# Squaring the second block's token rows two feature tiles after their load, at a fixed place in ScalarE's order

## The chip, the cores and the metric

The kernel runs on one core of a Trainium2 chip. The metric is the device time of one execution in microseconds (us); of several runs of a kernel the median counts. The engines are named as the profile names them: PE is TensorE (matrix products), PEld its weight loads, DVE is VectorE, ACT is ScalarE, POOL is GpSimd, SP is SyncE, which here issues all transfers (its rows read SPq). Each engine works through its own list of instructions in order and waits on semaphores for the others.

## The reference

One layer of a diffusion backbone is computed for 128 context tokens and 2048 latent tokens, of 1024 features each, in float32. Cut to what matters here:

```python
h = rmsnorm(x, norm_mix) * (1.0 + sc1) + sh1          # adaLN-modulated norm of each token row
proj = h @ w_in                                       # q, k, v (512 each), gate, betas and decays, gMLP parts
qkv = silu(centred_conv(proj[..., :1536], conv))      # 3-tap convolution along the tokens
q, k = l2norm(q per head), l2norm(k per head)         # 4 heads of 128
o_a  = gated delta rule over chunks of 64, both directions
o_b  = gelu(u) * (spatial mixing of layernorm(gelu(vg)))
x = x + ga1 * (concat(o_a, o_b) @ w_out)
x = x + ga2 * (relu(rmsnorm(x) * (1 + sc2) + sh2 @ w_ff1) ** 2 @ w_ff2)
y = rmsnorm(x, norm_final)
```

The norm needs, for each token row, the sum of the squares of its 1024 features. That sum is what the change moves.

## The kernel before

The 17 tiles of 128 tokens are worked off in phases. The **first phase** (to about 430 us) makes q, k and v of all tokens, their convolution and the products k k^T and q k^T; then follow the scans of the delta rule with the gMLP part and the output projection, and from about 1200 us the feed-forward part. Products that must be exact are made three times: an operand is split into a rounded part (names in H) and a rest (names in L), and `mm3` issues H*H, L*H and H*L (lines 241 to 243).

The first phase goes through six **blocks** of three tiles (the last has two): `BLOCKS`. Within a block there are twelve **feature tiles**, each 128 of the 1536 q, k and v features for all 384 tokens of the block: 24 matmuls into one PSUM bank (`pj`, three banks), then the convolution (`convolve`: a scaled copy on ACT at L568 and two multiply-adds on DVE at L571 read the bank, then a tanh on ACT at L574 and a product on DVE at L575 into a tile x2), one step later a transposition on PE (L584, into one of three banks `pt`) and its evacuation on ACT (squares at L595 and L601, a copy at L588), and later further transposes and products (L614, L625, L628).

Beside the matmuls of feature tile n of a block, side steps for the **next block** are issued. They are listed by `prep_block`, one entry of its list `first` per feature tile:

- entries 0 to 2, `load_x`: allocate one of three buffers with the tag x, load one tile of token rows (512 KB, L462) and at once issue the square with its row sum on ACT (L467, `junk<-x`);
- entries 3 to 5: `columns_r` (the inverse root of the sums and a diagonal matrix of it), `rows_r` (a product with ones that spreads it over the partitions, L481, copied at L484), and the loads of three pairs of transposed feature rows (`load_pair`, L491, 384 KB each, into the same three buffers with the tag x, so each waits until the square has read its buffer);
- entries 7 to 11 of the feature tiles: `column(k)` for the eight k. Each scales a feature row (DVE, L526), rounds it (ACT, L528, kH) and takes the rest (DVE, L529, kL). A fourth pair is loaded with column 2. Feature tiles of the next block multiply exactly these kH and kL.

So the first block's feature tiles stand beside the preparation of the **second block** (bi == 1 in `prep_block`), the second block's beside the third's, and so on. Beside all this run the casts and differences of the weights (`split_w`, L201 and L202; the v weights are loaded through a ring of four buffers) and the multiply-adds for the modulation vectors (L271, `acc`).

The code gives the steps in program order (`interleave` spreads the side steps evenly between the matmuls). The order of each engine's list is then made by the tile framework's scheduler, which estimates when each instruction could start and puts the lists in that order; it also deals out the rotating buffers. So a step that is written elsewhere can move rows on every engine for some distance behind it. `tc.add_manual_dep` with `NoSync` is a constraint on that scheduler only: one instruction has to stand behind another of the same engine.

## Time and profile before

| what | value |
|---|---|
| runs | 2576.61 us median of 3 (2570.27 to 2578.84) |
| the profiled execution | 2574.76 us, of which the span of its instructions is 2573.0 us |
| PE busy | 2536.3 us of 2573.0 (99%), 15268 matmuls |
| DVE, ACT, POOL busy | 1830.8, 1260.1 and 229.3 us |
| granted TensorE clock, mean | 0.998 |
| transfers | 588.66 MB, 229 GB/s on average |

A row of the timeline gives the start in us from the span's beginning, the duration, the engine, the line, the operation, output<-input without buffer numbers, sizes, and in brackets how long the engine had been idle before and who ended that idle time. Consecutive rows of one kind are merged (x3), and the start of the next row of an engine tells when it took up new work; the durations overlap a little, since an engine overlaps the end of one instruction with the start of the next. A row of windows gives for one stretch its length and then the busy time of PE, PEld, DVE, ACT and POOL with instruction counts, the granted clock, the busy share of the transfer engines and the rate. A row of waits gives the engine and what it waited to do, who released it, the total, the number of times and the longest.

### The profile page before, as it was taken

To read this page: it belongs to the slowest core of one execution; us is meant where nothing else is said; L and a number is where in the kernel's file an instruction comes from. 1 tells how busy PE (TensorE), PEld (TensorE's weight loads), DVE (VectorE), ACT (ScalarE), POOL (GpSimd) and SP (SyncE) were. 2 spreads that over 40 slices of the span, in tenths; PEclk is the share of its full clock that TensorE was granted. 3 is DMA by queue.
4 is the path that set the end of the run, shared out by engine and by line. 5 is a ranking of instruction groups with operands and counts; after the bars stand their busy time and mean duration, and the time that the engine had idled before them with its cause. 6 is when DMAs were issued, how large, how long until landed. Compare 5 with 4: busy or idle time off the path is not lost.

```text
span 2573.0 us, 44472 instructions
## 1 busy us (share of the span) xinstructions
PE 2536.3 (99%) x15268; PEld 2136.7 (83%) x15268; DVE 1830.8 (71%) x3790; ACT 1260.1 (49%) x3119; POOL 229.3 (9%) x448
## 2 busy tenths in 40 slices
PE   9999999999999999999999999999999999999998
PEld 5999999788888788778888888888888887888887
DVE  5867756776676878885678877777675556785875
ACT  4755556555555767763355544444342433243442
POOL 3112212211110111110000000000000000000000
PEclk9999999999999999999999999999999999999999
DMA  8977737744445657785867789665589979776673
GB/s 286 310 215 212 212 114 245 248 160 148 145 155 166 213 190 247 253 280 183 292 199 245 238 281 348 195 180 172 146 272 374 334 263 314 256 258 205 221 264 112
DMA packets 503912, 588.66 MB, mean 229 GB/s; under 512 B 36148, under 2 KB 298588, under 8 KB 500102
## 3 DMA queue, kind: packets, MB, share of 16 engines
q1 hardware_dynamic: 503686, 585.82, 69.7%
q8 instruction: 120, 1.97, 0.3%
q14 instruction: 106, 0.87, 0.1%
HBM read 406.01 MB, written 179.67 MB: 228 GB/s over the span
## 4 chain that ended last, share of the span: by engine, by line
PE 56%; DVE 3%; DMA 3%; ACT 1%; issue 1%; SPq 0%; POOL 0%; POOLq 0%; DVEq 0%; ACTq 0%
PE f L243 16%; PE f L241 16%; PE f L242 16%; PE pd L1026 2%; PE pj L241 1%; PE pj L242 1%; PE pj L243 1%; DMA QK<-qk_d 1%; DMA raw<-in_w_ff_dram 1%; DVE opL L904 0%; DMA kT<-kT_d 0%; DMA h_d<-ev 0%; DVE o L1358 0%; DVE KK L1067 0%; DMA zraw<-z_d 0%
## 5 line engine op out<-in xcount | busy, mean ns | idle before, releaser
L243 PE MATMUL f<-hop,zL 128*128 128x512 f32 (+1 forms) x976 | 377.0, 387 | 1.8 <-DVE zL L1551 1.8
L241 PE MATMUL f<-hop,zH 128*128 128x512 f32 (+1 forms) x976 | 376.9, 387 | 1.2 <-ACT zH L1557 1.2
L242 PE MATMUL f<-hop,zH 128*128 128x512 f32 (+1 forms) x976 | 376.7, 386 | 0.0
L241 PE MATMUL f<-hop,wH 128*128 128x512 f32 x896 | 349.7, 391 | 1.6 <-ACT p L1630 1.6
L242 PE MATMUL f<-hop,wH 128*128 128x512 f32 x896 | 348.7, 389 | 0.0
L243 PE MATMUL f<-hop,wL 128*128 128x512 f32 x896 | 347.3, 389 | 0.0
L1557 ACT CAST zH<-zraw 128x512 fp32r<-128x512 f32 x240 | 146.8, 620 | 295.6 <-DVE zraw L1551 84.2
L243 PEld LDWEIGHTS f<-hop,zL 128*128 128x128 f32 x976 | 183.6, 188 | 39.5 <-DVE zL L1551 3.0
L241 PEld LDWEIGHTS f<-hop,zH 128*128 128x128 f32 x976 | 183.7, 188 | 38.7 <-ACT zH L1557 1.6
L242 PEld LDWEIGHTS f<-hop,zH 128*128 128x128 f32 x976 | 183.7, 188 | 37.7 <-DVE hop L1551 0.3
L1551 DVE TENSOR_TENSOR zL<-zraw,zH 128x512 fp32r<-128x512 f32 x240 | 163.3, 689 | 68.8 <-ACT zH L1557 55.7
L241 PEld LDWEIGHTS f<-hop,wH 128*128 128x128 f32 x896 | 168.2, 188 | 37.3 <-ACT p L1630 3.1
L243 PEld LDWEIGHTS f<-hop,wL 128*128 128x128 f32 x896 | 168.2, 188 | 35.5
L242 PEld LDWEIGHTS f<-hop,wH 128*128 128x128 f32 x896 | 168.3, 188 | 34.6
L241 PE MATMUL pj<-kH,wH 128*128 128x386 f32 (+2 forms) x568 | 190.5, 338 | 1.8 <-ACT junk L601 1.1
L243 PE MATMUL pj<-kH,wL 128*128 128x386 f32 (+2 forms) x568 | 189.7, 335 | 0.0
L242 PE MATMUL pj<-kL,wH 128*128 128x386 f32 (+2 forms) x568 | 189.4, 335 | 0.0
L184 POOL TENSOR_TENSOR r<-rsq,nhalf 128x1 f32<-128x1 f32 (+1 forms) x37 | 23.0, 622 | 1398.1 <-DVE rsq L183 1398.1
L571 DVE SCALAR_TENSOR_TENSOR cv<-pj,vec,cv 128x384 f32<-128x384 f32 (+2 forms) x164 | 87.1, 540 | 53.3 <-ACT cv L568 52.0
L1557 ACT CAST wH<-s 128x512 fp32r<-128x512 f32 x96 | 59.4, 621 | 124.7 <-DVE s L1551 118.2
L241 PEld LDWEIGHTS pj<-kH,wH 128*128 128x128 f32 x568 | 107.1, 189 | 5.3 <-issue 2.1
L202 DVE TENSOR_TENSOR wL<-raw,wH 128x512 fp32r<-128x512 f32 x120 | 81.1, 685 | 38.8 <-ACT wH L201 38.6
(423 smaller groups left out, 5793.6 us busy)
## 6 DMA issues: line engine op xcount, KB each, us to landing
zraw<-z_d SPq DMA_DIRECT2D x212, 256.0 KB
raw<-in_w_ff_dram SPq DMA_DIRECT2D x192, 256.0 KB
hop<-hop_d SPq DMA_DIRECT2D x28, 1024.0 KB
z_d<-c SPq DMA_DIRECT2D x96, 256.0 KB
zraw<-s_d SPq DMA_DIRECT2D x96, 256.0 KB
raw<-in_w_mod_dram SPq DMA_DIRECT2D x80, 256.0 KB
r<-in_w_ff_dram SPq DMA_DIRECT2D x80, 256.0 KB
s_d<-s SPq DMA_DIRECT2D x64, 256.0 KB
```

The source lines that it names most:

```text
L184: G.tensor_tensor(out=out, in0=t[:np_, :n], in1=nhalf[:np_, :n], op=ALU.pow)
L202: V.tensor_tensor(out=lo, in0=raw, in1=f32(h), op=ALU.subtract)
L241: T.matmul(ps, lh, rh, start=first and i == 0, stop=False, skip_group_check=more)
L242: T.matmul(ps, lh, rl, start=False, stop=False, skip_group_check=more)
L243: T.matmul(ps, ll, rh, start=False, stop=last and i == n - 1, skip_group_check=more)
L571: V.scalar_tensor_tensor(out=cv[:, o : o + m], in0=ps[:, s + sh : s + sh + m], scalar=convw[:, w, j : j + 1], in1=cv[:, o : o + m], op0=AL ...
L1026: T.matmul(p[:, h, :], lhs[:, h, :], rhs[:, h, :], start=True, stop=True)
L1551: V.tensor_tensor(out=out, in0=a, in1=b, op=op)
L1557: A.copy(h, src)
```

## The change

For the second block alone (bi == 1) the square is taken out of `load_x`. Its three squares become steps of their own: the first stands at the third feature tile of the first block, in the same step as the third load; the second and third stand at the fourth and fifth. `columns_r`, `rows_r` and the pair loads, which come behind them in the list, thereby move two feature tiles on. In addition each of the three squares is bound to stand behind the ACT instruction that was emitted last before it in the program. For all other blocks the square follows its load as it did.

```diff
@@ load_x, in prep_block
                 load(out=x, in_=xrow(t))
-                if t == tiles[0]:
+                rows.append(x)
+                if bi > 1:
+                    square(t - tiles[0])
+
+            rows = []
+
+            def square(i):
+                if i == 0:
                     xs.append(smp.tile([P, 3], F32, tag="ss3", name="xss"))
-                i = t - tiles[0]
+                last = [x for x in tc.nc.cur_bb.bb.instructions if x.engine == mybir.EngineType.Activation][-1]
                 junk = p1.tile([P, D], BF16, tag="junk", name="junk", bufs=1)
-                A.activation(junk, x, AF.Square, accum_out=xs[0][:, i : i + 1])
+                A.activation(junk, rows[i], AF.Square, accum_out=xs[0][:, i : i + 1])
+                if bi == 1:
+                    tc.add_manual_dep(tc.nc.cur_bb.bb.instructions[-1], last.name, mybir.DependencyInfo(
+                        mybir.DependencyClass.NoSync, mybir.DependencyReason.DATA), reason="order")
...
             first = [lambda t=t: load_x(t) for t in tiles]
+            if bi == 1:
+                last_x = first[2]
+                first = first[:2] + [lambda: (last_x(), square(0)), lambda: square(1), lambda: square(2)]
             if bi:
                 first += [lambda: (columns_r(), load_pair(0)), lambda: (rows_r(), load_pair(1)), lambda: load_pair(2)]
```

No instruction is added or removed. What moves is shown at three places, by each engine's list. The line numbers of the changed kernel are 10 to 13 higher behind the edit (the square is its L474); the numbers behind the names count the buffers.

**ACT, beside the first block's fourth to sixth feature tiles.** cv is the convolution's input, copied out of its bank; x2 the tanh; wH the cast of a v weight that was loaded into raw; junk_... xss the square of token rows; junk2 the square of transposed features. Before:

```order
L574 ACTIVATE x2_845<-cv_844 128x384
L467 ACTIVATE junk_857,xss_856<-x_854 128x1024
L568 ACTIVATE cv_981<-pt_567,vec_195 128x128
L568 ACTIVATE cv_981<-pt_567,vec_195 128x256
L574 ACTIVATE x2_920<-cv_919 128x384
L467 ACTIVATE junk_914,xss_856<-x_912 128x1024
L568 ACTIVATE cv_1079<-pj_1009,vec_195 128x128
L201 CAST wH_949<-raw_947 128x512
L568 ACTIVATE cv_1079<-pj_1009,vec_195 128x256
```

Changed:

```order
L587 ACTIVATE x2_845<-cv_844 128x384
L581 ACTIVATE cv_977<-pt_567,vec_195 128x128
L581 ACTIVATE cv_977<-pt_567,vec_195 128x256
L587 ACTIVATE x2_915<-cv_914 128x384
L581 ACTIVATE cv_1069<-pj_1005,vec_195 128x128
L581 ACTIVATE cv_1069<-pj_1005,vec_195 128x256
L201 CAST wH_944<-raw_942 128x512
L587 ACTIVATE x2_978<-cv_977 128x384
L201 CAST wH_953<-raw_951 128x512
L614 ACTIVATE junk2_928,ss3_929<-pt_924 128x128
L474 ACTIVATE junk_972,xss_971<-x_854 128x1024
```

The first square has moved nine rows down, behind the casts of two v weights; the copies of the third and fourth feature tiles now stand first.

**ACT, where the second block's feature tiles begin.** kH_1629, 1644, 1659 and 1674 are the rounded columns 4 to 7 of the second block; x_1725, x_1795 and x_1859 the third block's token rows. Before:

```order
L528 ACTIVATE kH_1629<-full_1628,b1_197 128x384
L528 ACTIVATE kH_1644<-full_1643,b1_197 128x384
L467 ACTIVATE junk_1797,xss_1727<-x_1795 128x1024
L595 ACTIVATE junk2_1367,ssq_188<-pt_1363 128x128
L467 ACTIVATE junk_1861,xss_1727<-x_1859 128x1024
L595 ACTIVATE junk2_1367,ssq_188<-pt_1363 128x128 x2
L595 ACTIVATE junk2_1414,ssq_188<-pt_1410 128x128 x3
L568 ACTIVATE cv_1698<-pj_1601,vec_195 128x128
L568 ACTIVATE cv_1698<-pj_1601,vec_195 128x256
L528 ACTIVATE kH_1659<-full_1658,b1_197 128x384
L528 ACTIVATE kH_1674<-full_1673,b1_197 128x384
```

Changed:

```order
L538 ACTIVATE kH_1644<-full_1643,b1_197 128x384
L474 ACTIVATE junk_1797,xss_1727<-x_1795 128x1024
L641 COPY ev_1547<-pt_1543 128x384
L641 COPY ev_1554<-pt_1550 128x384
L601 COPY tk_1585<-pt_1581 128x384
L601 COPY tk_1692<-pt_1688 128x384
L587 ACTIVATE x2_1699<-cv_1698 128x384
L538 ACTIVATE kH_1659<-full_1658,b1_197 128x384
L474 ACTIVATE junk_1861,xss_1727<-x_1859 128x1024
L538 ACTIVATE kH_1674<-full_1673,b1_197 128x384
```

Column 4's cast (kH_1629) now stands four rows above these, behind the square of x_1725; the square of x_1795 stands ahead of columns 6 and 7, and that of x_1859 between them. In the changed kernel x_1795 is also given the buffer that x_1725 had (its load waits for ACT), where before it had another (its load waited for DVE).

**DVE, at the same place.** full is the scaled column, kL its rest, acc the modulation's multiply-adds; the copy kTt_1427 frees a bank that PE's transposes need. Before, ending with that copy and what follows it:

```order
L529 SCALAR_TENSOR_TENSOR kL_1630<-full_1628,b1_197,kH_1629 128x384
L529 SCALAR_TENSOR_TENSOR kL_1645<-full_1643,b1_197,kH_1644 128x384
L571 SCALAR_TENSOR_TENSOR cv_1591<-pj_1525,vec_195,cv_1591 128x128
L571 SCALAR_TENSOR_TENSOR cv_1591<-pj_1525,vec_195,cv_1591 128x256
L392 TENSOR_TENSOR mrow_1611<-pm_830,mrow_1611 2x512
L615 COPY kTt_1427<-pt_1428 128x384
L526 SCALAR_TENSOR_TENSOR full_1658<-xT_1492,a1_196,rrow_1117 128x384
L526 SCALAR_TENSOR_TENSOR full_1673<-xT_1492,a1_196,rrow_1117 128x384
```

Changed, ending with the same copy:

```order
L539 SCALAR_TENSOR_TENSOR kL_1565<-full_1563,b1_197,kH_1564 128x384
L392 TENSOR_TENSOR mrow_1611<-pm_830,mrow_1611 2x512
L271 SCALAR_TENSOR_TENSOR acc_1621<-raw_1837,scond_204,acc_1621 128x512
L536 SCALAR_TENSOR_TENSOR full_1628<-xT_1343,a1_196,rrow_1252 128x384
L584 SCALAR_TENSOR_TENSOR cv_1698<-pj_1601,vec_195,cv_1698 128x128
L271 SCALAR_TENSOR_TENSOR acc_1622<-raw_1837,scond_204,acc_1622 128x512
L584 SCALAR_TENSOR_TENSOR cv_1591<-pj_1525,vec_195,cv_1591 128x256
L628 COPY kTt_1427<-pt_1428 128x384
```

At the copy the changed list has scaled only column 4, where before columns 4 and 5 were finished and 6 and 7 came next; more of the modulation's multiply-adds stand ahead instead. On PE the matmuls of the second block's first two feature tiles and of the decay columns (L645, L646) are accordingly taken in turns, column by column.

## The prediction

> **What bounds the kernel now.** I read the page's first lines, then busy time by windows, then who PE waited for, and last the timelines of the engines at those waits. In this fence: the page's span and busy time, and windows of 100 and of 20 us.
>
> ```profile
> span 2573.0 us, 44472 instructions
> PE 2536.3 (99%) x15268; PEld 2136.7 (83%) x15268; DVE 1830.8 (71%) x3790; ACT 1260.1 (49%) x3119; POOL 229.3 (9%) x448
> 200.00:300.00 100.00, 100.00 (x639) 96.78 (x638) 72.19 (x143) 57.06 (x176) 17.74 (x41) 1.00 0.71 213
> 60.00:80.00 20.00, 17.71 (x104) 16.64 (x103) 12.88 (x36) 13.54 (x43) 0.86 (x1) 1.00 0.94 317
> 80.00:100.00 20.00, 20.00 (x123) 19.16 (x122) 18.77 (x42) 16.51 (x54) 3.67 (x3) 1.00 0.79 226
> 100.00:120.00 20.00, 20.00 (x128) 19.36 (x128) 16.58 (x35) 13.38 (x39) 8.25 (x33) 1.00 1.07 351
> ```
>
> PE sets the time: it is busy 2536.3 of 2573.0 us, and in the first phase nearly without a gap (100.00 of 100 us from 200 to 300). So what PE idles less near the start ends the kernel earlier by as much, and what it idles more ends it later. Beside the first block, from 60 to 80 us, it idles 20.00 - 17.71 = 2.29 us; from 80 to 120 us not at all. These are the gaps, and what ACT and DVE do just before:
>
> ```profile
> 71.08 0.52 PE L584 MATMUL pt<-ident,x 128*128 128x128 f32 x3 [0.84 <-DVE ab L656]
> 72.79 0.52 PE L584 MATMUL pt<-ident,x 128*128 128x128 f32 x3 [0.31 <-DVE x L575]
> 74.44 0.41 PE L241 MATMUL pj<-kH,wH 128*128 128x388 f32 x1 [1.13 <-ACT junk L601]
> 60.90 0.52 ACT L574 ACTIVATE x<-cv 128x384 f32<-128x384 f32 x1 [1.23 <-DVE cv L571]
> 66.98 1.06 ACT L467 ACTIVATE junk<-x 128x1024 bf16<-128x1024 f32 x1 [5.56 <-DMA x<-in_x_sample_dram]
> 68.04 0.71 ACT L568 ACTIVATE cv<-pt,vec 128x128 f32<-128x128 f32 x2
> 68.79 0.35 DVE L571 SCALAR_TENSOR_TENSOR cv<-pt,vec,cv 128x128 f32<-128x128 f32 x1 [6.38 <-ACT cv L568]
> ```
>
> The first square of the second block stands in ACT's list ahead of the third feature tile's copy and waits 5.56 us for its transfer. DVE then waits 6.38 us for that copy, and PE, a little later, 0.84 + 0.31 + 1.13 = 2.28 us for banks and tiles that DVE frees late. This is all that the square's wait costs: 2.28 us, 0.09% of the time.
>
> **Term A: the wait at 61 us.** The square is no longer there. The transfers behind it are the same and stand in the same order: token rows at 62.77, a modulation weight, token rows, then the v weights whose casts now stand ahead of the square.
>
> ```profile
> 62.77 0.44 SPq L462 DMA_DIRECT2D x<-in_x_sample_dram  x1
> 63.30 0.40 SPq L377 DMA_DIRECT2D raw<-in_w_mod_dram  x1
> 63.80 0.38 SPq L462 DMA_DIRECT2D x<-in_x_sample_dram  x1
> 64.23 0.97 SPq L190 DMA_DIRECT2D raw<-in_w_in_dram  x2
> 67.00:70.00 3.00, 3.00 (x19) 2.91 (x17) 1.15 (x4) 3.00 (x6) 0.00 (x0) 1.00 1.02 374
> 70.41 0.60 ACT L201 CAST wH<-raw 128x512 fp32r<-128x512 f32 x1
> 59.01 0.34 PE L241 MATMUL pj<-kH,wH 128*128 128x388 f32 x1
> 59.19 0.34 PE L242 MATMUL pj<-kL,wH 128*128 128x388 f32 x1
> ```
>
> ACT is free at 60.90 + 0.52 = 61.4. It copies the third tile (0.71) and makes a tanh (0.52), then copies the fourth tile, whose 24 matmuls start at 59.01, 0.177 us apart (59.01 to 59.19), and end near 63.5: done at about 64.3. Next in its list is the cast of a v weight. Between the landing of the first token rows (66.98) and of that weight lie 256 + 512 + 256 KB, 1.05 MB, at 374 GB/s 2.8 us: 69.8 (not after 70.41, where the cast ran without waiting). So ACT waits again, about 5.5 us, on another transfer. The wait is moved, not removed. What comes early is the third and fourth tile's copy. DVE's list interleaves the fourth tile's multiply-adds with the differences of two v weights, so that tile's bank comes free only at about 69.8 + 0.6 + 0.5 + 0.6 (two casts and a tanh between them), 0.7 for the second difference and 0.5 for the last multiply-add: 72.7. PE wants it, without the first two gaps and with three transposes (0.25) moved behind, at 74.44 - 1.13 - 0.84 - 0.31 + 0.1 = 72.2. A gap of 0.5 stays. **A = -2.28 + 0.5 = -1.8 us**, between -2.28 (no gap stays) and 0 (the cast's wait costs PE what the square's did).
>
> [...]
>
> **Term B: the second block's columns.** The inverse roots and the pair loads now come two feature tiles later, and with them all eight columns. Before, the early columns had time to spare and the last had none:
>
> ```profile
> 88.81 1.14 DVE L526 SCALAR_TENSOR_TENSOR full<-xT,a,rrow 128x384 f32<-128x384 f32 x2
> 108.99 0.33 PE L241 MATMUL pj<-kH,wH 128*128 128x386 f32 x1
> 112.06 0.56 DVE L615 COPY kTt<-pt 128x384 f32<-128x384 f32 x1
> 113.40 1.13 ACT L528 ACTIVATE kH<-full,b 128x384 fp32r<-128x384 f32 x2
> 115.57 1.14 DVE L529 SCALAR_TENSOR_TENSOR kL<-full,b,kH 128x384 fp32r<-128x384 f32 x2
> 116.19 0.55 PE L242 MATMUL pj<-kL,wH 128*128 128x386 f32 x2
> 125.19 0.41 PE L241 MATMUL pj<-kH,wH 128*128 128x386 f32 x1 [0.25 <-DVE cv L571]
> ```
>
> Columns 0 and 1 were scaled at 88.81 and first used at 108.99, 20 us on; ten later is harmless. Columns 6 and 7 were cast at 113.40, their rests begun at 115.57, and PE used the first of these at 116.19, at once. In the changed lists these two stand behind two squares of the third block, whose loads wait for buffers that the second block's columns free late. The price of such a load is in these rows:
>
> ```profile
> 95.70 0.70 SPq L462 DMA_DIRECT2D x<-in_x_sample_dram  x1
> 101.43 1.06 ACT L467 ACTIVATE junk<-x 128x1024 bf16<-128x1024 f32 x1 [1.64 <-DMA x<-in_x_sample_dram]
> 102.69 0.91 SPq L462 DMA_DIRECT2D x<-in_x_sample_dram  x2
> 108.47 1.06 ACT L467 ACTIVATE junk<-x 128x1024 bf16<-128x1024 f32 x1 [1.41 <-DMA x<-in_x_sample_dram]
> 116.63 1.41 DVE L271 SCALAR_TENSOR_TENSOR acc<-raw,scond,acc 128x512 f32<-128x512 f32 x2
> ```
>
> From issue to square 101.43 - 95.70 = 5.7 and 108.47 - 102.69 = 5.8 us, with the transfer engines full (share 1.07). I take 5.8. Step by step:
>
> - PE reaches the second block at 108.99 - 1.8 (A) - 0.8 (nine transposes that now come after) = 106.4.
> - The load of x_1725 is issued behind the store of column 3, which is cast just before the last feature tile ends: about 105.5. Square from 111.3 to 112.4. Column 4's cast follows.
> - x_1795 has the same buffer, so its load is issued at 112.5, its square runs from 118.3 to 119.4. Behind it in ACT's list stand two copies ev, two copies tk, a tanh (five at 0.45 to 0.5) and column 6's cast: 122.0. Then the square of x_1859 (its load is long there), 123.0, column 7's cast, 123.6, and its rest on DVE, 124.2.
> - DVE alone gives nearly the same end: between the copy kTt and column 7's rest now stand eight modulation multiply-adds (1.41 / 2 = 0.70 each: 5.6), seven column operations (0.57 each: 4.0), and 2.1 of convolution work, 11.7 us, where it was 115.57 + 1.14 - 112.06 = 4.7. With the copy at 112 as before, 123.8.
> - PE stops at the transposes that wait for the bank emptied by the first ev copy, 119.9. From there to the third feature tile it has 16 matmuls, three of column 6, five or six of column 7, three groups of transposes and small products, and the ends: about 7 us, 126.9. Before, this point was 125.19, and 0.65 us of the modulation's small products now lie ahead of it that came later before.
>
> So at that point the change stands at 126.9 - 125.19 - 0.65 = **+1.1 us, A and B together; B alone +2.9**. What hides it up to there is the second feature tile and the decay columns, which PE takes in turns with the first; with columns 6 and 7 missing all three are stuck, and no fourth bank is there. Bounds of B: 0, if the turns cover all; +6, if each of the two loads in a row takes 1.5 us longer than 5.8.
>
> [...]
>
> **Term C: everything behind.** The scheduler also exchanges rows in the later blocks and, a few, in the scans and the feed-forward part. PE idles little there:
>
> ```profile
> PE f L243 <- DVE zL L1551: 1.8, 1, 1.8
> PE f L241 <- ACT p L1630: 1.6, 3, 0.7
> ```
>
> No wait of the feed-forward part sums to over 1.8 us. I take C = 0, give or take 1.8. In the third block the columns are again later, but its first columns have a like slack, and eight multiply-adds have been done early, so I expect no gap.
>
> **Sum.** -1.8 + 2.9 + 0 = +1.1 us. The profiled execution took 2574.76 us, 1.85 below the median of the runs (2576.61); with +1.1 it would take 2575.9, and the median of such runs 2577.7. I forecast **2577.5 us**: no change that can be told, which for this kernel takes about 0.3%, 7.7 us.
>
> **The rivals.**
>
> *The wait is simply gone.* The v weights land in time, or PE does not mind, and the columns' delay is hidden: A = -2.28, B = 0, 2574.3 us. For it: 20 us of slack in the early columns, and ACT idles half of the time. Against it: the order of the transfers, and no slack at 116.19. It is within 0.3% too.
>
> *The loads in a row decide.* The loads of x_1725 and x_1795 run one behind the other through one buffer. If the columns' stores, the modulation weights and the stores of keys in front of each (five of 256 KB, 3.5 us at 374 GB/s) come first, each takes 9.3 us. Then the copy that PE waits for ends at 126.9 instead of 119.9, PE is stuck from 112 on, and the total is +1.1 + 7.0 = +8.1: 2584.7 us, slower. It decides from the moment at which the square of x_1795 ends after 119.4, and from there each us costs one. For it: share 1.07 from 100 to 120 us. Against it: 5.8 us were measured under that very share.
>
> *The change does not do what it says.* ACT's list has the square's wait replaced by the cast's and PE keeps its three gaps, while the columns are hidden: 0, 2576.6 us.
>
> **Chances.** My sum (+1.1, with B between 1 and 5) 0.55; the wait gone 0.22; nothing moved 0.13; the loads in a row 0.10, of which 0.06 beyond 7.7 us. All but the last stay within 0.3%; C and the runs' own scatter (-6.3 to +2.2 about their median) may push a case over on either side by about 0.04 each. So faster by over 0.3%: 0.05; within: 0.86; slower: 0.09. The range goes from the gain at its bound less some scatter, 2571, to the far bound of B with A, 2576.6 - 1.8 + 6 = 2580.8, and some scatter: 2583.
>
> **What would show it.** In the changed kernel's profile: A right, if ACT's long wait before 70 us is at a cast from raw (about 5.5 us) and PE's gaps from 60 to 80 us fall below 1 us. B right, if PE idles 2 to 4 us between 108 and 128 us, with waits on ACT's copies ev or on kH and kL, and ACT waits for x before a square near 118. B is wrong, if PE is full there, and the time falls by 2 us; the forecast fails if PE idles over 8 us there, or if a gap of several us opens in a later block or at the start of the scans that no row of before announces.

## The result, and the profile after

| | before | changed |
|---|---|---|
| median of the runs | 2576.61 us (9 runs) | 2585.04 us (9 runs) |
| the profiled execution | 2574.76 us | 2582.47 us |

The ratio of the times is 1.004, with a 95% interval from 1.0025 to 1.0055: 6 to 14 us slower. Timed a second time beside other kernels (the last of the runs below) it was 1.0039, 1.0024 to 1.0053. One of the changed kernel's nine runs was disturbed (4623.76 us at a mean clock of 0.773); its median has that run in it, the ratio leaves it out. The forecast was 2577.5 us in a range up to 2583.

The page's span and busy time of the changed kernel, and its windows of 20 us, columns as before (PE, PEld, DVE, ACT, POOL, the granted clock, the share of the transfer engines, GB/s):

```profile
span 2580.7 us, 44444 instructions
PE 2537.2 (98%) x15268; PEld 2138.5 (83%) x15268; DVE 1831.4 (71%) x3790; ACT 1260.3 (49%) x3119; POOL 232.6 (9%) x448
60.00:80.00 20.00, 17.26 (x93) 16.58 (x92) 12.50 (x31) 13.15 (x39) 1.09 (x1) 0.91 0.92 296
100.00:120.00 20.00, 17.44 (x106) 17.05 (x105) 19.07 (x38) 11.87 (x36) 10.65 (x33) 0.91 0.97 298
120.00:140.00 20.00, 17.34 (x114) 15.80 (x113) 14.72 (x29) 7.82 (x17) 0.00 (x0) 1.00 1.00 315
```

PE still idles beside the first block's middle (2.74 of 20 us, 2.29 before). New are 2.56 us from 100 to 120 and 2.66 from 120 to 140 us, where before had one gap of 0.25. Two more numbers have changed: DVE is busy 19.07 of 20 us from 100 to 120 us (16.58 before), and the granted clock is 0.91 in two windows where it was 1.00. Whom PE waited for between 55 and 140 us:

```profile
PE pj L241 <- DVE ab L670: 2.7, 1, 2.7
PE pt L597 <- ACT ev L641: 2.6, 1, 2.6
PE pj L241 <- DVE absb L661: 2.2, 1, 2.2
PE pj L241 <- ACT kH L538: 0.5, 1, 0.5
```

**The first gap.** The timeline around 70 us:

```profile
68.72 0.62 ACT L201 CAST wH<-raw 128x512 fp32r<-128x512 f32 x1 [5.80 <-DMA raw<-in_w_in_dram]
71.82 0.47 DVE L584 SCALAR_TENSOR_TENSOR cv<-pj,vec,cv 128x256 f32<-128x256 f32 x1
72.21 0.19 DVE L670 TENSOR_TENSOR ab<-ab,pt 128x48 f32<-128x48 f32 x1
72.44 0.42 PE L241 MATMUL pj<-kH,wH 128*128 128x388 f32 x1 [2.74 <-DVE ab L670]
```

ScalarE's long wait stands at the cast of a v weight, 5.80 us, where term A put it, and the fourth tile's last multiply-add ends at 71.82 + 0.47 = 72.3 (72.7 was forecast). But PE stood there from 72.44 - 2.74 = 69.70 on, not from 72.2.

**The second place.** The timeline from 108 to 133 us, SyncE's loads of token rows, ScalarE, VectorE and PE together:

```profile
108.73 0.71 SPq L462 DMA_DIRECT2D x<-in_x_sample_dram  x1
113.78 1.06 ACT L474 ACTIVATE junk<-x 128x1024 bf16<-128x1024 f32 x1 [1.98 <-DMA x<-in_x_sample_dram]
113.79 0.55 DVE L628 COPY kTt<-pt 128x384 f32<-128x384 f32 x1
114.84 0.46 ACT L641 COPY ev<-pt 128x384 f32<-128x384 f32 x1
115.35 0.90 PE L597 MATMUL pt<-ident,x 128*128 128x128 f32 x3 [2.56 <-ACT ev L641]
119.86 0.59 SPq L462 DMA_DIRECT2D x<-in_x_sample_dram  x1
123.73 0.56 DVE L588 SCALAR_TENSOR_TENSOR x<-x,cv 128x384 f32<-128x384 f32 x1 [1.27 <-ACT x L587]
125.92 1.06 ACT L474 ACTIVATE junk<-x 128x1024 bf16<-128x1024 f32 x1 [1.72 <-DMA x<-in_x_sample_dram]
126.98 0.60 ACT L538 ACTIVATE kH<-full,b 128x384 fp32r<-128x384 f32 x1
127.61 0.62 DVE L539 SCALAR_TENSOR_TENSOR kL<-full,b,kH 128x384 fp32r<-128x384 f32 x1 [1.47 <-ACT kH L538]
129.42 1.18 DVE L286 TENSOR_TENSOR mrow<-pm,mrow 2x128 f32<-2x128 f32 x4 [1.19 <-PE pm L280]
131.12 0.88 DVE L269 TENSOR_SCALAR acc<-raw,scond 128x512 f32<-128x512 f32 x2 [0.52 <-DMA raw<-in_w_mod_dram]
132.03 0.55 DVE L661 COPY absb<-pj 32x384 f32<-32x384 f32 x1
132.63 0.44 PE L241 MATMUL pj<-kH,wH 128*128 128x386 f32 x1 [2.21 <-DVE absb L661]
```

The first square waits 1.98 us for its load, the copy ev behind it empties a bank, and PE has stood 2.56 us for that bank. Column 7's cast stands behind the square of x_1859, whose load was issued only at 119.86, and its rest begins on DVE at 127.61. Behind it, still ahead of the copy absb, DVE ends one modulation row (L286) and begins the next (L269), with waits of 1.19 and 0.52 us. From the copy kTt (113.79) to absb (132.03) VectorE's list takes 18.2 us, of which 13.7 are work and 4.45 are waits: for a tanh (1.27), for column 7's cast (1.47), and those two. PE waits 2.21 us for absb, and its third feature tile of the second block starts at 132.63: 125.19 before, 126.9 in the forecast.

**A cost that the forecast had not at all: the clock.** Windows of the changed kernel on a grid of 3.41 us:

```profile
70.43:73.84 3.41, 1.40 (x8) 1.43 (x9) 3.29 (x10) 3.41 (x13) 0.00 (x0) 1.00 0.92 306
73.84:77.25 3.41, 3.41 (x14) 3.31 (x13) 3.10 (x8) 3.41 (x11) 1.09 (x1) 0.50 0.89 270
111.39:114.80 3.41, 1.40 (x12) 1.13 (x10) 3.38 (x8) 1.40 (x5) 2.97 (x12) 1.00 1.01 329
114.80:118.21 3.41, 2.86 (x10) 2.86 (x11) 3.41 (x8) 2.69 (x8) 0.00 (x0) 0.50 0.73 218
```

Behind each of the first two gaps the granted clock is 0.50 for 3.41 us. If PE's work takes twice as long in it, half of such a stretch is lost at most: 3.41 x 0.50 = 1.7 us, an estimate. By the matmuls it is a little less: in the first stretch those of 128x388 start 0.32 us apart (75.95 and 76.27), behind it 0.18 (77.79 and 77.97), which makes 1.5 us. PE counts as busy for 3.41 of 3.41 us in it, so no idle time shows the loss.

### The profile page after: what moved, and what is told of

Its sections match the earlier page's. It is cut to its first block, busy times and chain, and to the rows that moved or that the text cites. A ratio compares the mean times of both kernels' runs of the same rounds, so it can differ in the third digit from the quotient of the medians.

```text
span 2580.7 us, 44444 instructions
## 1 busy us (share of the span) xinstructions
PE 2537.2 (98%) x15268; PEld 2138.5 (83%) x15268; DVE 1831.4 (71%) x3790; ACT 1260.3 (49%) x3119; POOL 232.6 (9%) x448
## 4 chain that ended last, share of the span: by engine, by line
PE 56%; DMA 3%; DVE 3%; ACT 1%; issue 1%; SPq 0%; POOL 0%; POOLq 0%; ACTq 0%; DVEq 0%
PE f L241 16%; PE f L243 16%; PE f L242 16%; PE pd L1039 2%; PE pj L241 1%; PE pj L242 1%; PE pj L243 1%; DMA raw<-in_w_ff_dram 1%; DMA QK<-qk_d 1%; DMA z_d<-c 0%; DMA hop<-hop_d 0%; DVE opL L917 0%; PE f L901 0%; DVE KK L1080 0%; DMA hop_d<-opL 0%
```

## The experiments

To compare profiles I cut each trace by PE's own count of matmuls, from 0. **Stretch 1** ends at the start of the 330th (near 79 us, behind the first gap). **Stretch 2** goes on to the 2500th (near 415 us) and holds the second place. In stretch 2 the matmuls themselves take 333 to 337 us in every profile, since some rows move over the cuts; the columns behind tell what comes on top. "Half clock" is half the length of the 0.50 stretches. Each time is put beside runs of the kernel before that were timed with it.

| kernel (one profile each) | 330th matmul at | stretch 2 lasts | PE idle in it | half clock in it | ratio to before, 95% interval |
|---|---|---|---|---|---|
| before | 78.97 | 334.25 | 0.25 | 0 | |
| before, again | 78.12 | 335.76 | 1.87 | 0 | |
| changed | 79.03 | 341.97 | 5.21 | 1.71 | 1.004 (1.0025 to 1.0055) |
| changed, again | 80.36 | 344.04 | 6.73 | 1.71 | |
| changed, timed again | 79.86 | 346.56 | 6.83 | 5.12 | 1.0039 (1.0024 to 1.0053) |
| delay only | 79.16 | 334.88 | 0.10 | 0 | 1.0015 (1.0006 to 1.0024) |
| squares only | 79.66 | 337.60 | 2.55 | 1.71 | 1.0024 (1.0014 to 1.0035) |
| squares only, v weights late | 77.03 | 341.59 | 4.95 | 0 | 1.0023 (1.0013 to 1.0033) |
| changed, no constraint | 79.68 | 346.67 | 6.72 | 5.12 | 1.0056 (1.0043 to 1.0068) |
| changed, third block's squares bound | 77.42 | 341.41 | 4.35 | 1.71 | 1.0015 (1.0006 to 1.0024) |
| the same, again | 78.95 | 341.35 | 4.18 | 1.71 | |
| squares bound, v weights late | 75.79 | 344.42 | 7.68 | 1.71 | 1.0034 (1.0021 to 1.0046) |
| squares bound, modulation late | 80.71 | 334.75 | 1.60 | 0 | 1.0018 (1.0009 to 1.0027) |
| modulation late alone | 79.97 | 334.34 | 1.41 | 0 | 0.9998 (0.9989 to 1.0007) |
| all three cures | 75.07 | 343.95 | 7.03 | 1.71 | 1.003 (1.0019 to 1.004) |
| before, third block's squares bound | 81.18 | 334.43 | 0 | 0 | 1.0012 (1.0003 to 1.0021) |

### Second profiles of both kernels

The changed kernel again, nothing edited:

> The changed kernel once more, for a second profile. Theory 'two gaps': the gap near 71 us (2.74 us, a conv bank freed late behind the cast of a v weight) and the gaps from 112 to 133 us (2.56 + 0.45 + 2.21 = 5.2 us) come again within 0.5 us each, since they follow from the order of the lists; each is followed by a stretch of about 3.4 us in which the granted clock is 0.5. Rival 'clock by chance': the gaps come again, but the half-clock stretches stand elsewhere or are missing, and the time moves by up to 1.7 us for each. Rival 'scatter': the gaps themselves move by over 1 us. The earlier start (PE 1.75 us ahead at 67 us) is expected again by the theory that it comes from the changed lists, and not by the rival that it is scatter of the start-up.

It took 2594.53 us. The gaps came again (3.1 us near 71 us; 2.9, 1.1 and 2.7 us at ev, kH and absb), in the same rows and mostly a few tenths longer. The half-clock stretches did not come by one for each gap: none behind the gap of 2.9 us, one behind the gap at absb, which had none in the first profile, and four in places that have none in the first profile (463, 1173, 1597 and 2491 us). So these gaps follow from the lists, and the clock's answer to them varies. The start, too, was half way between: PE's 247th matmul at 61.41 us, after 60.44 in the changed kernel's first profile and 62.19 before.

The kernel before again:

> The kernel before once more, for a second profile. The question is what of the differences between single profiles is scatter. In the first profile of before PE idled 1.58 us up to its 247th matmul, 2.29 in three pieces up to 79 us, 0.25 from there to 130 us, and 15.5 us (with one half-clock stretch) in the scans from 604 to 1173 us; the changed kernels idled 18 to 20.5 us in the scans. Theory: the gaps up to 130 us come again within 0.5 us (they follow from the lists), and the scans' idle is scatter: 17 to 20 us this time. Rival: the scans' rows moved by the change cost 3 us: 15 to 16 us again.

It took 2571.36 us. PE's waits between 55 and 140 us, and the first square's row:

```profile
PE pt L625 <- ACT junk L595: 1.7, 1, 1.7
PE pj L241 <- ACT junk L601: 0.3, 1, 0.3
```

```profile
65.63 1.06 ACT L467 ACTIVATE junk<-x 128x1024 bf16<-128x1024 f32 x1 [2.73 <-DMA x<-in_x_sample_dram]
```

The gaps of before did not come again: 0.31 us in place of 2.28 near 73 us, and 1.73 us at 112 us, where the first profile had none. The square waited 2.73 us, not 5.56: PE and ScalarE had come 1.5 us later through the start (a half-clock stretch at 29 us), and the load landed 1.4 us sooner, at 65.6. The 330th matmul came at 78.12, not later than the 78.97 of the first profile. **What was lost at the start was won back at the load, whose landing sets the pace here.** From 604 to 1173 us, in the scans, PE idled 18.6 us, as in my theory, and 15.9 in the first profile by the same window: most of what the changed kernels idled more there lies within the scatter of the kernel before.

The changed kernel, timed beside the last kernels and with a third profile:

> The changed kernel once more, timed beside the others and with a third profile. Theory: 8 to 11 us above before; PE idles 5 to 7 us from 79 to 140 us at the copy ev, at kH and at absb; at 70 to 75 us one gap of 1.7 to 3.5 us; a half-clock stretch stands behind every grid window of 3.413 us in which PE idled over 2.0 us, and none behind a window with less than 1.4 us.

Measured: 2585.15 us against 2575.27 us before, 9.9 us more. PE's waits:

```profile
PE pt L597 <- ACT ev L641: 3.5, 1, 3.5
PE pj L241 <- DVE absb L661: 3.0, 1, 3.0
PE pj L241 <- ACT cv L581: 2.6, 1, 2.6
```

These are the same three places for the third time. One half-clock window came against my rule: it followed a window with only 0.68 us of idle, which itself ran at half clock.

### One half of the change at a time

The delay without the squares: two empty steps, the squares stay with their loads.

```diff
             first = [lambda t=t: load_x(t) for t in tiles]
+            if bi == 1:
+                first += [lambda: None, lambda: None]
```

> The squares stay with their loads, without the order tie; only the inverse roots, the spread and the pair loads of the second block come two feature tiles later (two empty steps in their place). Theory 'late columns': the whole loss of the first phase comes from this part: PE idles 4 to 6 us between 108 and 135 us, waits on ev, kH, absb, and the time is 6 to 8 us above before: 2583 to 2585. The gaps of before at 70 to 75 us (2.3 us) are still there. Rival 'the tie or the squares': full PE from 80 to 140 us, 2576.6 give or take 2. Rival 'both halves': 2579 to 2581, half the loss.

```profile
100.00:120.00 20.00, 20.00 (x129) 19.61 (x129) 17.23 (x35) 12.26 (x36) 10.59 (x32) 1.00 1.06 330
120.00:140.00 20.00, 20.00 (x119) 19.34 (x119) 15.74 (x34) 12.54 (x42) 3.37 (x4) 1.00 0.84 274
```

My theory "late columns" falls: PE is full from 80 to 140 us, and stretch 2 is as long as before. Two tiles of delay alone are hidden. The runs were 2578.09 us against 2573.17, 4.9 us more. In the profile (2578.16 us) stretches 1 and 2 don't show them; behind the 2500th matmul it took 2155.6 us, where before took 2153.0 and 2149.0. Whether that comes from the delay or is scatter, one profile can't tell.

The squares without the delay:

```diff
-                first = first[:2] + [lambda: (last_x(), square(0)), lambda: square(1), lambda: square(2)]
-            if bi:
-                first += [lambda: (columns_r(), load_pair(0)), ...]
+                first = first[:2] + [lambda: (last_x(), square(0)),
+                                     lambda: (square(1), square(2), columns_r(), load_pair(0))]
+            elif bi:
+                first += [lambda: (columns_r(), load_pair(0))]
+            if bi:
+                first += [lambda: (rows_r(), load_pair(1)), lambda: load_pair(2)]
```

> Only the squares are moved and tied; inverse roots and pair loads of the second block are at the same feature tiles as before. Theory 'late columns': PE is full from 80 to 140 us; near 71 us the gap of 2.7 us and, behind it, the half-clock stretch stay, so the first phase is 0 to 2 us longer than before and the time 2576 to 2579. Rival 'the tie or the squares': 2583 to 2585, with gaps beyond 100 us. Rival of the forecast's term A: a gap below 1 us near 71 us and 2574 to 2575.

In this edit the third square also stands one feature tile sooner than in the changed kernel. The kernel took 2579.9 us against 2573.17. The first gap and its half-clock stretch stayed, as expected. Not expected was a gap of 2.55 us at 127 us:

```profile
126.78 0.48 ACT L644 COPY ev<-pt 128x384 f32<-128x384 f32 x1 [3.23 <-DMA kk_d<-ev]
127.31 0.55 PE L600 MATMUL pt<-ident,x 128*128 128x128 f32 x3 [2.55 <-ACT ev L644]
```

The copy ev waits 3.23 us for the store that empties its buffer, a new wait and none of mine. So neither half alone makes the gaps of the changed kernel in stretch 2; they come from both together. The times alone would not tell that: 1.0015 for the delay and 1.0024 for the squares add up to the changed kernel's 1.0039.

Without the constraint:

```diff
-                if bi == 1:
-                    tc.add_manual_dep(tc.nc.cur_bb.bb.instructions[-1], last.name, ...)
```

> The change without the order constraint: squares, inverse roots and pair loads stand where the change put them, the scheduler alone orders the squares. Theory: the constraint is not the cause; the square of x_1725 still stands ahead of the copy ev, so the gap of 2 to 3 us near 113 us stays, and the time is 8 to 11 us above before, as the changed kernel. Rival 'the tie costs it': under 1 us idle from 80 to 140 us and 2 to 4 us above before, as with the delay alone.

It took 2586.5 us against 2572.25: the constraint is not the cause. PE's longest waits between 55 and 145 us:

```profile
PE pj L241 <- DVE ab L667: 2.7, 1, 2.7
PE pj L241 <- ACT kH L535: 2.3, 1, 2.3
PE pt L635 <- ACT junk L605: 2.1, 1, 2.1
```

The gap near 114 us stayed, but PE waited there for a square of transposed features, not for ev; the place is the same, the last releaser is another.

### The first gap

The v weights one feature tile later, with the squares alone:

```diff
-                if bi == 0 and 2 <= n <= 5:
-                    side += wv[2 * n - 4 : 2 * n - 2]
+                if bi == 0 and 3 <= n <= 6:
+                    side += wv[2 * n - 6 : 2 * n - 4]
```

> As the run with the squares alone, and the loads and casts of the v weights one feature tile later, so that no cast that waits stands ahead of the fourth feature tile's tanh. Theory: the gap near 71 us goes (below 0.5 us) and with it the half-clock stretch: 4.4 us less than with the squares alone, 2.3 us less than before: 2572 to 2575, at the edge of what can be told. Rival 'something else is late next': another wait of 2 us or more between 60 and 100 us takes its place and the time is 2576 to 2579.

It does what it should in stretch 1: the 330th matmul 2 to 3 us sooner (77.03), 1.48 us of idle, no half-clock stretch. Stretch 2 takes it back and more (341.59, with 4.95 us of idle, in waits for cv, ev and kn). That the later casts and differences of the v weights make these waits is likely, but not shown. The time was 2579.85 us against 2573.17, just above the rival's range.

### The second place

The third block's squares bound behind what precedes them in the program, in the changed kernel:

```diff
-                if bi == 1:
+                if bi in (1, 2):
                     tc.add_manual_dep(tc.nc.cur_bb.bb.instructions[-1], last.name, ...)
```

> The changed kernel, and the third block's squares are bound too, so that on ScalarE they stand behind the casts of columns 6 and 7 and the copies ev; up to that place every engine's list is that of the changed kernel. Theory 'third block's squares': the gaps of 2.56, 0.45 and 2.21 us from 112 to 133 us fall to 1.5 us or less in sum and the half-clock stretch at 115 us goes: 5 to 7 us less than the changed kernel, 3 to 5 us above before. The gap at 71 us (2.7 us) and the half-clock stretch behind it stay. Rival 'DVE alone' (eight multiply-adds and the column operations between the copy kTt and column 7's rest): the gaps move but sum to 4 us or more, and the time is that of the changed kernel.

```profile
125.63 0.48 DVE L269 TENSOR_SCALAR acc<-raw,scond 128x512 f32<-128x512 f32 x1 [1.48 <-PE pj L243]
127.89 0.75 DVE L271 SCALAR_TENSOR_TENSOR acc<-raw,scond,acc 128x512 f32<-128x512 f32 x1 [1.77 <-DMA raw<-in_w_mod_dram]
128.56 0.54 DVE L661 COPY absb<-pj 32x384 f32<-32x384 f32 x1
129.15 0.69 PE L241 MATMUL pj<-kH,wH 128*128 128x386 f32 x1 [3.18 <-DVE absb L661]
```

The gap at ev went, but 4.35 us of idle stayed, 3.18 of them in one piece, where DVE has two modulation operations with waits of 1.48 and 1.77 us ahead of absb: the rival's row. The time is the theory's all the same, 2575.58 us against 2572.25, 3.3 us more. The profiled execution took nearly that (2576.18 us): it made up for part of stretch 2 with an early 330th matmul (77.42) and a short remainder (2148.8 us behind the 2500th). A second profile was to tell whether the gap varies:

> The changed kernel with the third block's squares bound, a second profile. Its runs were 6 us faster than the changed kernel's, but its profile idled nearly as much from 77 to 132 us (4.35 us and one half-clock stretch; matmuls 330 to 2500 in 341.4 us, where before took 334 to 336 and the changed kernel 342 to 347). Theory: the place varies from run to run with the landing of a modulation weight, and this profile takes 335 to 339 us for those matmuls. Rival: 341 us or more again, and the gain lies elsewhere.

It doesn't: 341.35 us for stretch 2 again, 3.1 us at absb again, and this run took 2584.02 us, outside the eleven runs of this same kernel that were timed first (up to 2580.38). That this binding gains 6 us, as its runs said, I don't hold for shown.

With both, the squares bound and the v weights late:

> As the run before it, and the loads and casts of the v weights one feature tile later. Theory: both places are cured, the gap at 71 us shrinks to 1.5 us without a half-clock stretch (as in the run of the squares with the v weights late), and 80 to 140 us has 1.5 us or less: within 1.5 us of before, on either side. Rival 'new waits take the places': 4 us or more of idle from 80 to 140 us, in other rows, and 5 us above before.

The first gap went (0.31 us, no half-clock stretch, 330th matmul at 75.79), but stretch 2 idled 7.68 us: the rival. The time was 2579.3 us against 2572.25, 7 us more.

Four modulation steps later, beside the bound squares:

```diff
-MOD_STEPS = (1, 1, 0, 0, 0, 1, 0, 2, 0, 1, 1, 2)
+MOD_STEPS = (1, 1, 0, 0, 0, 1, 0, 2, 0, 1, 1, 0)
...
-                nm = MOD_STEPS[n] if bi == 0 else n != 6
+                nm = MOD_STEPS[n] if bi == 0 else n != 6 and not (bi == 1 and n < 2)
```

> The changed kernel with the third block's squares bound behind the columns, and four modulation steps (two at the first block's last feature tile, one each at the second block's first two) taken out of this stretch and done later in the list. Theory 'VectorE is late next': in the run with the squares bound, the copy absb stood behind two multiply-adds that waited 1.48 us for PE and 1.77 us for a modulation weight, and PE waited 3.2 us for it; with that work gone from ahead of absb PE idles 1.5 us or less from 80 to 140 us, no half-clock stretch stands there, and the time is 2 to 4 us under that run, 0 to 2 us above before. Rival 'it is the transfers, not VectorE': absb or another row waits for columns or loads all the same, 3 us or more of idle, no gain on that run.

```profile
100.00:120.00 20.00, 19.77 (x130) 19.39 (x129) 18.50 (x39) 12.04 (x41) 10.18 (x33) 1.00 0.97 288
120.00:140.00 20.00, 18.63 (x121) 17.18 (x120) 18.55 (x37) 10.79 (x28) 0.00 (x0) 1.00 1.07 353
```

There are 1.60 us of idle in place of 4.2 to 4.4 and no half-clock stretch, and stretch 2 takes 334.75 us, as before. VectorE's work from kTt to absb is what it was with the squares bound alone (12.7 us against 12.8); its waits there fell from 3.25 to 0.7 us. So what the steps cost ahead of absb was their waits, in a list that is worked off in order. The runs took 2575.09 us against 2570.86, no better than with the squares bound alone; in this profile the first gap had grown to 3.5 us with a half-clock stretch.

The modulation steps later, and the squares not bound:

> The changed kernel with only the four modulation steps later; the third block's squares stand ahead of the copies ev and of columns 6 and 7, as in the changed kernel. Theory 'both are needed': the gap at the copy ev and a wait on column 6 or 7 stay, 3 to 5 us of idle from 79 to 140 us and at least one half-clock stretch, 4 to 8 us above before. Rival 'VectorE alone': 2 us of idle or less there, as with both cures, and 2 to 4 us above before.

It took 2572.93 us against 2574.19: **0.9998, the loss is gone.** Its windows, the three squares that wait for their loads, the first of these loads, column 7's cast, and absb:

```profile
100.00:120.00 20.00, 18.89 (x121) 17.85 (x120) 17.95 (x38) 12.27 (x40) 10.22 (x33) 1.00 0.99 291
120.00:140.00 20.00, 20.00 (x132) 19.18 (x132) 17.63 (x35) 10.70 (x30) 0.00 (x0) 1.00 1.01 328
```

```profile
110.46 1.12 SPq L462 DMA_DIRECT2D x<-in_x_sample_dram  x1
116.41 1.06 ACT L474 ACTIVATE junk<-x 128x1024 bf16<-128x1024 f32 x1 [2.45 <-DMA x<-in_x_sample_dram]
121.40 1.06 ACT L474 ACTIVATE junk<-x 128x1024 bf16<-128x1024 f32 x1 [1.41 <-DMA x<-in_x_sample_dram]
124.13 0.62 ACT L538 ACTIVATE kH<-full,b 128x384 fp32r<-128x384 f32 x1
126.79 1.06 ACT L474 ACTIVATE junk<-x 128x1024 bf16<-128x1024 f32 x1 [2.04 <-DMA x<-in_x_sample_dram]
127.41 0.54 DVE L661 COPY absb<-pj 32x384 f32<-32x384 f32 x1
```

ScalarE waits for the three squares 2.45 + 1.41 + 2.04 = 5.9 us, longer than in the changed kernel, and the first load takes 116.41 - 110.46 = 5.95 us from issue to square. Neither makes PE wait much: 1.41 us of idle. The copy absb comes at 127.41, not at 132.03. So the rival "VectorE alone" named the result, and my theory that both cures are needed falls. The edit does more than one thing, though. Ahead of absb only a modulation row's end and two operations are gone (16 operations on acc stand ahead of it, as before, and 18 in the changed kernel); from kTt to absb VectorE works 12.5 us without a wait, where the changed kernel had 13.7 us of work and 4.45 of waits. The four steps also take four loads of 256 KB away from here; that the loads of token rows were no quicker speaks against the transfers as the reason. And the scheduler now puts column 7's cast (124.13) ahead of the third square (126.79), where the changed kernel has it behind (126.98). How much of the gain is that cast's, this run alone doesn't tell. With the squares bound, the cast stands ahead of the square with and without the late modulation; there the modulation steps alone took away 2.6 to 2.75 us of idle and the half-clock stretch.

All three cures together:

> All three cures on the changed kernel: the third block's squares bound behind the columns, the four modulation steps later, and the loads and casts of the v weights one feature tile later. So far a late v weight brought PE's 330th matmul to 76 to 77 us (78 to 81 in the kernel before and in the changed one), and the other two cures brought the 2170 matmuls behind it to 334.8 us, as before. Theory: both add up, 2 to 4 us less than before: 2567 to 2569 where before has 2571. Rival 'the v weights' casts crowd the next stretch': they fall between 80 and 120 us, where the run with two of these cures idled 4 to 5 us; then no gain, 1 to 5 us above before.

The 330th matmul at 75.07 us, the best of all, and stretch 2 in 343.95. PE waits 1.1 us for a v weight's cast near 86 us, and the last difference of a v weight starts on DVE at 95.23. So it is not with these that DVE is busy 19.43 of 20 us from 100 to 120 us, but with columns, convolution and modulation; and a modulation row's end and the next one's begin (L286 at 126.43, L269) stand ahead of absb again, which comes at 130.48. The time was 2582.86 us against 2575.27, 7.6 us more: no gain, as the rival said, but beyond its 1 to 5 us and only in part for its reason. No kernel here beats the kernel before beyond its interval.

### The same binding in the kernel before

```diff
+                last = [x for x in tc.nc.cur_bb.bb.instructions if x.engine == mybir.EngineType.Activation][-1]
                 A.activation(junk, x, AF.Square, accum_out=xs[0][:, i : i + 1])
+                if bi == 2:
+                    tc.add_manual_dep(tc.nc.cur_bb.bb.instructions[-1], last.name, ...)
```

> The kernel before, with only the third block's squares bound behind the copies and casts that precede them in the program. Theory: before loses 0.25 to 1.9 us from 79 to 130 us, so at most that much can be won: within 2 us of before. Rival: pushing the third block's squares back delays its loads and columns, as the change did for the second block: 3 to 7 us slower, with idle time of PE after 130 us.

It took 2574.54 us against 2570.86, 3.7 us more: the rival's time, without the rival's idle, for stretch 2 has none at all. Its lists are those of before up to 101 us, and yet it had gaps of 1.5, 0.9 and 1.1 us there and a half-clock stretch behind them: a third draw of the first gap, beside 2.28 and 0.31.

## Why the prediction was wrong

**Term A (-1.8 us) was not won.** The cast's wait (5.80 us, "about 5.5") and the bank (72.3, forecast 72.7) came as worked out. The step that failed is "PE wants it at 72.2": it took one execution's arrival for fixed, and it left out the clock. Three draws with the lists of before have the 330th matmul at 78.97, 78.12 and 81.18 us (mean 79.4; the third is the kernel before with the binding). The changed kernel has it at 79.03, 80.36 and 79.86, and four more profiles with its lists up to 103 us (squares bound, twice, and modulation late, with and without the binding) at 77.42, 78.95, 80.71 and 79.97: 79.5 in the mean of the seven. So A is 0.1 us, not -1.8, with single draws up to 3 us apart.

The landing of the transfers sets the pace. In six of these seven profiles the 330th matmul comes 10.1 to 10.3 us after the start of the v weight's cast that ScalarE waits for, whenever that is (68.65 to 70.61 us); in the seventh, the only one without a half-clock stretch behind the gap, it comes after 8.7 us. PE goes on behind its last gap 1.2 us sooner than before in the means (73.2 against 74.4 us), but the half-clock stretch stands there in six profiles of seven, against one of three, and three transposes have moved behind. The rival "the change does not do what it says" had this half right. One reading of the term was also wrong: the third gap of before, 1.13 us, was ended by ScalarE (junk), not by DVE.

**Term B (+2.9 us) was mis-sized: stretch 2 took 344.2 us in the mean of three profiles, 335.0 in the mean of before's two, +9.2 us.** Idle time and half clock make up 8.0 of it: 9.1 against 1.1 in the means of the table. By its steps:

- "issued at about 105.5": 108.73; the square then ended at 114.84, not 112.4. The copy ev behind it cost PE 2.56 us up to 115.35, and later copies and columns cost more; the forecast had one stop, ended by a copy at 119.9.
- "x_1795 ... to 119.4": 120.1, close. The first two loads were faster than 5.8 us (113.78 - 108.73 = 5.1 for the first).
- "x_1859 (its load is long there)" is the failed step on ScalarE: that load was issued at 119.86, and column 7's cast came at 126.98, not near 123.
- "DVE alone gives nearly the same end" is the step that the runs single out. From the copy kTt to the end of column 7's rest the forecast had 11.7 us of work, and that is what it was; but it took 14.4 us (113.79 to 128.23), since 1.27 and 1.47 of waits are in it that the term put at nothing, and the copy itself came 1.7 us later than "at 112 as before". And the term stopped at that rest. Behind it the list had a modulation row's end and the next one's begin ahead of absb, with two more waits, 3.8 us in all, on which PE's third bank hung. The forecast had counted eight multiply-adds ahead of the rest, and had booked PE's small products of the modulation as a gain ("0.65 us ... now lie ahead of it"), but had nothing behind the rest. With four of the steps taken out absb comes at 127.4 to 128.3 us, as before (127.9), and stretch 2 is as long as before, with the loads as slow as ever.

**The rival "the loads in a row decide" named the right time, 2584.7 us, by the wrong cause, which is luck.** It needed 9.3 us for each load; in the changed kernel none took over 6.1 from issue to square.

**Term C (0, give or take 1.8)** holds but for one profile: from the 2500th matmul to the last before took 2153.0 and 2149.0 us, before with the binding 2151.5, the changed kernel 2152.6, 2161.3 and 2152.0; the 2161.3 has four half-clock stretches in it (6.8 us). A and B alone make 0.1 + 9.2 = 9.3 us; the medians lie 8.4 us apart in the first timing and 9.9 in the second.

**The clock was left out.** Mean clocks of 0.998 before and after hid it: two half-clock stretches each ahead of the one at the end, but in other places, at 1159.95 and 2187.36 us before and at 73.84 and 114.80 us after.

The bounds failed with the step: "+6, if each of the two loads takes 1.5 us longer" bounded the loads, not the waits in DVE's list, so 2583 was too low.

**What stays open:** three kernels whose stretch 2 is as before (the delay only, the squares bound with the modulation late, and the kernel before with the binding) ran 1.2 to 1.8 per mille slower than before, 3 to 5 us, while the modulation steps alone did not. Their profiles have a half-clock stretch at the first gap (1.7 us), but so has that of the modulation steps alone; single profiles don't settle it. Nor do the times follow stretch 2 throughout: with the squares bound it was 6.4 us longer than before in both profiles, and with the modulation late as well it was as before, yet the runs of the two lie 3.3 and 4.2 us above theirs. Only where the modulation alone was late did the loss go in the runs too. Why both halves together let the scheduler put the columns so far behind the modulation work was read from the lists, not tried.

## What to carry to other kernels

When a step is moved in a kernel whose engine lists are made by a scheduler, follow each engine that the moved work passes through to the point where the bounding engine takes something from it, and not only to the last moved row: here VectorE's list had one more modulation row ahead of the copy that PE needed. Add up the waits in such a list and not only its work: the work was forecast right, and the waits were the cost. Moving a wait that ends with a transfer won nothing here, since the next row waited for the same stream of transfers: ScalarE's wait of 5.56 us at the square became one of 5.80 us at a cast. Profile the kernel twice before a gap of 2 us is taken for a fixed one: 2.28 us in one profile of the kernel before were 0.31 in the next. And price a gap of the bounding engine with the clock: in the changed kernel, 3.41 us at a clock of 0.50 followed each of the two gaps that had 2.0 us in one window of 3.41 us, by the estimate above up to 1.7 us more for each.

## What the runs showed of the hardware

Not expected: **the half-clock stretches of a profile stood on one grid.** In each of the 15 profiles that have such a stretch ahead of the one at the end, the starts of all stretches with a granted clock of 0.5 were whole multiples of 3.4133 us apart, to within 0.001 of a step: in the first profile of before 1159.95, 2187.36 and 2569.65 us, 301 and 112 steps apart, in that of the changed kernel 73.84, 114.80 and 2575.81 us, 12 and 721 steps apart. What went with them was PE's idle time within one window of this grid, in one piece or several (in the kernel before with the binding a stretch followed two pieces of 0.91 and 1.13 us). Of the windows of the 16 profiles after the first 5 us that ran at full clock themselves, all 19 with 2.0 us of idle or more were followed by a half-clock window; of 63 with 1.4 to 2.0 us 13 were, and what decides among these is open; of 107 with 0.9 to 1.4 us none. In the first profiles of the two kernels alone, ahead of the stretch at the end, it was 2 of 2, 2 of 8 and 0 of 13. Behind two windows that ran at half clock themselves, with 0.68 and 1.00 us of idle, the clock stayed at a half. So of two gaps of like length one was followed by a half-clock stretch and the other not, as they lay on the grid. The changed kernel's gap of 2.74 us left 2.0 us in one window (70.43 to 73.84 us), and the clock in the next was 0.50. The gap of 2.9 us in its second profile was cut in two, 1.25 us in the window up to 115.39 us and 1.68 us in the next, and no half-clock stretch followed (this window is the second part, 1.73 of 3.41 us busy, and the clock in the next was 1.00):

```profile
115.39:118.80 3.41, 1.73 (x11) 1.73 (x12) 3.41 (x8) 3.29 (x8) 0.95 (x5) 1.00 0.82 203
118.80:122.21 3.41, 3.41 (x27) 3.41 (x26) 3.41 (x8) 1.55 (x4) 0.00 (x0) 1.00 0.98 318
```

The kernel before had 2.28 us in three pieces over 4.2 us, 1.44 us at most in one window (71.10 to 74.52 us), and kept its clock.

A second point is the start. Gaps at the first transfers came and went from run to run (PE idle 0.1 to 1.9 us up to the 247th matmul in the sixteen profiles). In the four profiles that have the first square ahead of the third tile's copy, ScalarE's wait for it answered to the start the other way: 7.06, 6.17, 5.56 and 2.73 us, with the 247th matmul at 60.91, 61.64, 62.19 and 63.67, since its load landed within 1.6 us of the same moment (65.6 to 67.2 us).
